# The sample's value block as fp32 on four column parts of TensorE, and GpSimd as the engine that normalizes the mLSTM's heads

## The chip, the core and the metric

The kernel runs on one core of one Trainium2 chip. The time is the device time of one execution in microseconds (us), as a median over runs. A core has TensorE (PE; its weight loads are listed apart, as PEld), VectorE (DVE), ScalarE (ACT), GpSimd (POOL) and SyncE (SP), which here issues the DMAs. Each engine works through its own instructions in a fixed order and waits on semaphores for the others.

## What is computed

The reference is one inference step of two trunk layers on a prompt of 1024 tokens and a sample block of 32 tokens, of width 1024. Layer 0 is an mLSTM mixer and an MLP, layer 1 chunk-band attention and an MLP. The change lies in layer 0's mixer, which has 4 heads with keys of 128 and values of 256:

```python
proj = u @ w_in
qk_pre = proj[..., :2 * QK_A]
v = proj[..., 2 * QK_A:2 * QK_A + V_A]
...
h, C, n, m = mlstm_scan(q, k, v, ig, lf, C0, n0, m0, chunk_len)
mu = h.mean(-1, keepdims=True)
var = jnp.square(h - mu).mean(-1, keepdims=True)
h = (h - mu) * lax.rsqrt(var + HEAD_NORM_EPS) * mhn_g
h = h.reshape(Bsz, S, V_A) * jax.nn.sigmoid(o_pre)
return h @ w_out, conv_new, C, n, m
```

Prompt and sample have states of their own, but share the weights, and so the kernel projects all 1056 tokens together.

## The kernel before

**Precision.** Most products run in fp32r, a faster form of fp32 on TensorE, on operands split into a high and a low part: `split` (line 87) casts on ScalarE (L89) and subtracts on VectorE (L90). A product then takes three matmuls, high by high, high by low and low by high. The modulated input u is kept in this way in the tile U, all channels of the high part, then of the low part, and 96 columns of zeros behind.

**Weights.** `wtile` loads 512 rows of a weight into a raw tile, of which there are three in a ring (`raw_tile`, line 84), by a DMA on SP's queue, and splits it into a w tile, of which there are six. A raw tile is free for the next load when both parts of the split have read it.

**Values.** The tokens are nine tiles: eight of 128 tokens of the prompt, and the sample's 32. `v_chunk` makes one eighth of a tile's product: the stationary operand is a block of u (128 channels by 128 tokens), the moving one 256 columns of the split weight, and three matmuls (L487 to L489) go into a PSUM bank. So a tile takes 24 matmuls. The sample's tile takes them too: its 32 tokens are read with the next 96 columns as a block of 128, and only 32 rows of the result are used. `v_out` copies the bank to a tile vt on ScalarE (L494). The nine vt tiles of a head reuse those of the head before. Head 0's values are made in `v_first` with 264 columns, of which the last eight are the gates. Those of heads 1 to 3 are made in `v_proj`, which loads both weight halves, then makes tile by tile, and calls `after(t)` behind each.

**The mLSTM.** `mlstm(h, ...)` is a generator that works in visits. It runs through the head's nine chunks (eight of the prompt, and the sample as chunk 8) while the next head's projections are made. In visit i, `scores(i)` makes S and the transposed keys, the decay weights W, the product sT (VectorE), the weighted keys kw (ScalarE) and the scaled queries qc (GpSimd, L675). `values(i - 1)` makes num (L686, L688) and the new state from cu (L690), takes the statistics of num on VectorE, and copies num to a tile hn on ScalarE (L708). After each third chunk, `scales` works out for three chunks together a scale and a shift, in some 13 short VectorE instructions on 128x3 (L715 to L727) with two on ScalarE between, and ScalarE applies them to the three hn tiles (L731). `heads(c)` transposes hn on TensorE (hT, L738) and copies it to G. `state_out` stores the final states. The heads of a trio are transposed in the visit behind the one that normalized them, and in the next.

**The order of work.** The projections call `flow.tick` behind each unit of theirs (`after_qk`, `tick`), and each tick makes the next visit of the mLSTM and the next step of other running tasks. For head 1 these are four ticks in `qk_proj` and nine in `v_proj`, for heads 2 and 3 six and nine; the last head's visits run in the twelve ticks of `o_proj([0, 1])`. The same ticks drive `ada_wide`, which works through the adaLN weights on VectorE (L279 and others) in steps. The order in which an engine meets its instructions is near the one in which they are written, but not equal to it: a scheduler puts ready instructions ahead of others that it expects to wait. So TensorE's transposes, say, stand between matmuls of a value tile.

**The conditioning vector** lies in cs, 32 columns for each of 8 blocks of channels, of which two are used. At the start, L435 multiplies cs in fp32 by the adaLN weight on four column parts of TensorE: the four results, 32 rows each, lie one below the other in one PSUM bank.

## Time and profile before

| | |
|---|---|
| median of 3 runs | 2409.23 us (2408.87 to 2410.61) |
| the profiled execution | 2412.41 us |
| its span, first to last instruction | 2410.6 us |
| mean granted TensorE clock | 0.995 |

The profile is of one execution. Its page gives busy time by engine; other views group instructions by line, list who waited for whom, list instructions in order of time, and give busy time by stretches of the span. In these rows stand the line of the code, the engine, the operation, the tiles written and read (`out<-in`), their shapes, the count (`x72`) and, in brackets, the idle time ahead and what ended it. A matmul's length holds its latency, so that successive ones overlap; what one costs is the distance between starts. In rows of stretches the figure behind the stretch's length is the busy time of each engine with its count of instructions, then the granted clock, the DMA engines' busy share and their GB/s. A row of waits has the total in us, the count and the longest.

### The profile page before, as it was taken

The numbers are of one execution on the slowest core, as the hardware profiler recorded it, in microseconds if no ns is written. First come the engines' busy times: TensorE is split into PE (matmuls) and PEld (weight loads), VectorE is DVE, ScalarE is ACT, GpSimd is POOL, SyncE is SP. The second block draws the span as 40 slices with busy tenths as digits, with TensorE's granted clock in tenths as the row PEclk, the third lists the DMA queues.
The fourth block names the chain that finished last, engine by engine and source line by source line (L and its number), as shares of the span: only waits on it lengthen the run. The fifth ranks groups of instructions, "written<-read, shape, count | busy, mean of one in ns | idle before, by whom it ended". The sixth has DMA issues, their size and how long they took to land. (4 is left out here: it accounts for less than half of the span.)

```text
span 2410.6 us, 44188 instructions
## 1 busy us (share of the span) xinstructions
PE 2342.7 (97%) x17180; PEld 2250.4 (93%) x17180; DVE 1939.0 (80%) x3903; ACT 1206.0 (50%) x2454; POOL 168.1 (7%) x320
## 2 busy tenths in 40 slices
PE   7999999999999999999999999999999999899997
PEld 4999999999999999999999987789999999899997
DVE  4888766778788789989888777756998889888778
ACT  4565557278666630101147467773776777222212
POOL 0111100000000000000000224420000000000003
PEclk9999999999999999999999999999999999999999
DMA  8343222526566896675512330051486779976642
GB/s 302 120 131 103 78 89 66 177 91 206 184 198 200 279 336 230 252 261 215 183 56 89 82 93 1 10 140 59 165 278 211 259 278 335 355 256 236 224 146 73
DMA packets 284277, 424.64 MB, mean 176 GB/s; under 512 B 15384, under 2 KB 205228, under 8 KB 278948
## 3 DMA queue, kind: packets, MB, share of 16 engines
q1 hardware_dynamic: 279860, 391.48, 48.3%
q10 hardware_dynamic: 4208, 30.35, 3.1%
q8 instruction: 135, 2.21, 0.4%
q14 instruction: 74, 0.61, 0.1%
HBM read 305.96 MB, written 118.17 MB: 176 GB/s over the span
## 5 line engine op out<-in xcount | busy, mean ns | idle before, releaser
L1082 DVE SCALAR_TENSOR_TENSOR ACX<-dn,ada,ACX 128x264 f32<-128x264 f32 (+6 forms) x664 | 281.8, 447 | 83.2 <-PE dn L1452 41.1
L1452 PE MATMUL dn<-fx,wf_d 128*128 128x264 f32 x2016 | 254.1, 285 | 6.8 <-DVE ACX L1082 3.5
L1452 PEld LDWEIGHTS dn<-fx,wf_d 128*128 128x128 f32 x2016 | 248.8, 188 | 9.0 <-DVE ACX L1082 3.0
L89 ACT CAST w_dn<-raw_dn 128x1024 fp32r<-128x1024 f32 x36 | 37.7, 1050 | 282.1 <-DVE aw L279 136.9
L118 PE MATMUL dn<-hs,w_dn 128*128 128x384 f32 (+2 forms) x512 | 161.2, 315 | 0.0
L119 PE MATMUL dn<-hs,w_dn 128*128 128x384 f32 (+2 forms) x512 | 161.0, 315 | 0.0
L120 PE MATMUL dn<-hs,w_dn 128*128 128x384 f32 (+2 forms) x512 | 156.4, 314 | 1.3 <-DVE w_dn L90 1.3
L1317 PE MATMUL up<-TF,wf_u 128*128 128x264 f32 x1056 | 143.2, 285 | 3.8 <-ACT H L1320 3.8
L1317 PE MATMUL up<-U,wf_u 128*128 128x264 f32 x1056 | 140.3, 285 | 1.7 <-ACT H L1320 1.2
L1317 PE MATMUL up<-u,wf_u 128*128 128x264 f32 x1056 | 139.7, 285 | 1.3 <-ACT wf_u L89 0.7
L279 DVE SCALAR_TENSOR_TENSOR aw<-radw,cs,aw 128x512 f32<-128x512 f32 x196 | 139.5, 743 | 1.1 <-DMA radw<-in_w_ada_dram 1.1
L1317 PEld LDWEIGHTS up<-TF,wf_u 128*128 128x128 f32 x1056 | 134.4, 189 | 4.8 <-ACT H L1320 4.6
L1317 PEld LDWEIGHTS up<-U,wf_u 128*128 128x128 f32 x1056 | 133.0, 188 | 3.0 <-ACT H L1320 1.6
L1317 PEld LDWEIGHTS up<-u,wf_u 128*128 128x128 f32 x1056 | 132.9, 188 | 1.9 <-ACT wf_u L89 0.9
L118 PE MATMUL dn<-U,w_dn 128*128 128x384 f32 (+2 forms) x416 | 129.4, 312 | 0.6 <-DVE ada L304 0.6
L119 PE MATMUL dn<-U,w_dn 128*128 128x384 f32 (+2 forms) x416 | 129.4, 312 | 0.0
L120 PE MATMUL dn<-U,w_dn 128*128 128x384 f32 (+2 forms) x416 | 125.9, 313 | 0.6 <-DVE w_dn L90 0.5
L1817 ACT ACTIVATE p<-p,mx 128x576 f32<-128x576 f32 (+9 forms) x132 | 86.6, 657 | 27.5 <-DVE mx L1814 25.2
L120 PEld LDWEIGHTS dn<-hs,w_dn 128*128 128x128 f32 x512 | 96.0, 188 | 2.0 <-DVE w_dn L90 1.8
L118 PEld LDWEIGHTS dn<-hs,w_dn 128*128 128x128 f32 x512 | 96.5, 189 | 0.1
L119 PEld LDWEIGHTS dn<-hs,w_dn 128*128 128x128 f32 x512 | 96.6, 189 | 0.0
L90 DVE TENSOR_TENSOR HL<-H,HL 128x1056 fp32r<-128x1056 f32 x64 | 80.3, 1254 | 20.0 <-ACT HL L89 19.9
(403 smaller groups left out, 7111.0 us busy)
## 6 DMA issues: line engine op xcount, KB each, us to landing
hpl<-HL SPq DMA_DIRECT2D x144, 264.0 KB
rdn_u<-in_w_up_dram SPq DMA_DIRECT2D x64, 512.0 KB
hd<-HL SPq DMA_DIRECT2D x28, 1056.0 KB
fx<-hd SPq DMA_DIRECT2D x50, 528.0 KB
radw<-in_w_ada_dram SPq DMA_DIRECT2D x24, 1024.0 KB
hd<-HM SPq DMA_DIRECT2D x28, 792.0 KB
raw_up<-in_w_up_dram SPq DMA_DIRECT2D x40, 512.0 KB
raw_dn<-in_w_down_dram SPq DMA_DIRECT2D x36, 512.0 KB
```

The lines of the kernel that those rows point to most:

```text
L89: nc.scalar.copy(dst_h, src)
L90: (eng or nc.vector).tensor_sub(dst_l, src, dst_h.bitcast(F32))
L118: nc.tensor.matmul(ps, wh, mov(0, k), start=(k == 0), stop=False)
L119: nc.tensor.matmul(ps, wh, mov(1, k), start=False, stop=False)
L120: nc.tensor.matmul(ps, wl, mov(0, k), start=False, stop=(k == nk - 1))
L279: nc.vector.scalar_tensor_tensor(acc[cnd], raw[:, k], sc, acc[cnd], op0=ALU.mult, op1=ALU.add)
L1082: nc.vector.scalar_tensor_tensor(xs, ps[:, off + o:off + o + mm_], gate[:, fc, cnd:cnd + 1], xs, op0=ALU.mult, op1=ALU.add)
L1317: nc.tensor.matmul(p, self.ws[w][:, wl, k], moving(f, tp, xl, k), start=first and k + n_ == 0, stop=k == 3 and n_ == 2, skip_group_check=n ...
L1452: nc.tensor.matmul(p, ws[w][:, wl, k], t[:, s0, xl], start=first and k + n_ == 0, stop=k == kg - 1 and n_ == 2, skip_group_check=not first)
L1817: nc.scalar.activation(z, z, AF.Exp, bias=mx[:, 0:1], scale=-1.0, accum_out=mx[:, 1:2])
```

## The change

For heads 1 to 3 the sample's values are no longer made from the split operands. The high and low parts of the sample's u are added once (`us`, on VectorE, behind head 0's values) into 32 further columns of cs, and `v_sample` multiplies them by the raw weights in fp32, as soon as a half of them is loaded and ahead of the split: four matmuls a half, each on one column part of TensorE, with 32 tokens stationary and 256 columns moving. The bank then holds four partial sums of 32 rows; ScalarE copies the first to vt, and VectorE adds the other three. These values stand ahead of the head's eight other tiles, in two vt tiles of their own. The ninth `after` follows the eighth at once.

Head 0's sample tile still uses the split operands, but with 32 tokens stationary, and so U loses its 96 columns of zeros. GpSimd applies scale and shift to hn in place of ScalarE. Each transposition stands one visit later, and within its visit ahead of `values`; the generator has 13 visits in place of 12. The constant `ones_d`, which the layer norms use, is made later, in another pool.

```diff
-            between()
+            between(raw)
         split(w[:, 0], w[:, 1], raw, eng)
...
-    cs = cp.tile([P, KC, 32], F32, name="cs")
+    cs = cp.tile([P, KC, 2 + TS], F32, name="cs")
+    us = cs[:, :, 2:]
...
-    U = upool.tile([P, 2 * UF + 96], F32R, name="U")
-    nc.vector.memset(U[:, 2 * UF:].bitcast(F32), 0.0)
+    U = upool.tile([P, 2 * UF], F32R, name="U")
...
     def v_chunk(ps, ws, t, k):
         w = ws[k // 4]
         n = w.shape[-1]
-        uh, ul = uap(0, k, t * P, P), uap(1, k, t * P, P)
+        m = P if t < NT - 1 else TS
+        uh, ul = uap(0, k, t * P, m), uap(1, k, t * P, m)
+        ps = ps[:m]
...
+    def v_sample(us, ps, half, raw):
+
+        for k in range(4):
+            nc.tensor.matmul(ps[32 * k:32 * k + 32, :256], us[:, 4 * half + k], raw[:, k], start=(half == 0),
+                             stop=(half == 1))
+
     def v_out(ps, h, t):
         m = P if t < NT - 1 else TS
-        vt = A.tile([P, 258], F32, tag="vt", name=f"vt_{h}_{t}", bufs=9)
+        vt = A.tile([P, 258], F32, tag="vt", name=f"vt_{h}_{t}", bufs=8) if m == P else \
+            A.tile([P, 258], F32, tag="vs", name=f"vt_{h}_{t}", bufs=2)
         nc.scalar.copy(vt[:m, :256], ps[:m, :256])
+        if m < P and h:
+            for q in range(1, 4):
+                nc.vector.tensor_add(vt[:m, :256], ps[32 * q:32 * q + m, :256], vt[:m, :256])
...
     def v_proj(h, after):
-        ws = [v_weight(h, half) for half in range(2)]
+        ps = mmt(f"v_{h}_s")
+        ws = [v_weight(h, half, lambda raw: v_sample(us, ps, half, raw)) for half in range(2)]
+        vs = v_out(ps, h, NT - 1)
         vts = []
-        for t in range(NT):
+        for t in range(NT - 1):
...
-        return vts
+        after(NT - 1)
+        return vts + [vs]
...
-                nc.scalar.activation(hn[:L], hn[:L], AF.Identity, bias=sm[:L, i, 7:8], scale=sm[:L, i, 6:7])
+                nc.gpsimd.tensor_scalar(hn[:L], hn[:L], sm[:L, i, 6:7], sm[:L, i, 7:8], op0=ALU.mult, op1=ALU.add)
...
-        for i in range(NT + 3):
+        for i in range(NT + 4):
             if i < NT:
                 scores(i)
+            if i >= 5 and i % 3 != 1:
+                for c in (i - 5, i - 4) if i % 3 == 2 else (i - 4,):
+                    heads(c)
             if 1 <= i <= NT:
                 values(i - 1)
             if 2 <= i < NT + 2:
                 state_out(i - 2)
-            if i >= 4 and i % 3:
-                for c in (i - 4, i - 3)[:3 - i % 3] if i % 3 == 1 else (i - 3,):
-                    heads(c)
             yield
...
+    uv = U.rearrange("p (i k t) -> p i k t", i=2, t=T)[:, :, :, TP:].bitcast(F32)
+    nc.vector.tensor_add(us, uv[:, 0], uv[:, 1])
...
+    ones_d = T_.tile([P, P], F32R, name="ones_d")
+    nc.vector.memset(ones_d.bitcast(F32), 1.0 / D)
```

## The prediction

> **What bounds the kernel now.** I read the totals first, then the stretches, then TensorE's waits. Heads are counted from 0, as in the names.

> ```profile
> span 2410.6 us, 44188 instructions
> PE 2342.7 (97%) x17180; PEld 2250.4 (93%) x17180; DVE 1939.0 (80%) x3903; ACT 1206.0 (50%) x2454; POOL 168.1 (7%) x320
> ```

> TensorE is busy for 97% of the span. The change touches the projections and the mLSTM, which end at about 390 us; so the next view is busy time by stretches.

> ```profile
> core 0: us, PE busy (x) PEld busy (x) DVE busy (x) ACT busy (x) POOL busy (x), PEclk, DMA share, GB/s
> 35.00:130.00 95.00, 92.20 (x610) 88.22 (x611) 81.02 (x157) 64.26 (x143) 13.90 (x30) 0.96 0.42 132
> 130.00:180.00 50.00, 48.68 (x343) 45.06 (x342) 42.26 (x107) 28.80 (x81) 8.79 (x22) 1.00 0.49 152
> 180.00:230.00 50.00, 48.65 (x337) 44.90 (x336) 44.51 (x109) 29.24 (x90) 8.65 (x30) 1.00 0.33 106
> 230.00:280.00 50.00, 49.78 (x340) 48.27 (x340) 41.93 (x86) 26.55 (x71) 5.42 (x16) 1.00 0.26 77
> 280.00:390.00 110.00, 108.73 (x697) 101.34 (x696) 70.88 (x194) 66.13 (x178) 8.43 (x23) 1.00 0.30 93
> 390.00:2411.00 2021.00, 1974.37 (x14768) 1916.19 (x14767) 1650.50 (x3232) 983.97 (x1884) 121.75 (x187) 1.00 0.54 184
> ```

> TensorE binds before 390 us and after it (1974 of 2021 us), where its order is unchanged. What TensorE saves early is thus saved at the end; what only ScalarE or GpSimd saves is not. The waits of TensorE and of its weight loads (PEld) between 35 and 390 us:

> ```profile
> PE hT L738 <- ACT hn L731: 3.5, 4, 1.3
> PE ae_ps L577 <- ACT stk L570: 2.4, 1, 2.4
> PE v L487 <- ACT U L378: 0.9, 1, 0.9
> PEld hT L738 <- ACT hn L731: 6.5, 11, 1.5
> ```

> Only one of them belongs to the change: the transposes hT wait for the heads hn that ScalarE normalizes (L731). One of the four of 3.5 us, by TensorE's timeline (start, length, and in brackets the idle time before it):

> ```profile
> 154.40 0.28 PE L487 MATMUL v<-w_v,U 128*128 128x256 f32 x1
> 155.87 0.44 PE L738 MATMUL hT<-ident,hn 128*128 128x128 f32 x2 [1.19 <-ACT hn L731]
> ```

> **The change part by part.** *Removed matmuls.* Heads 1 to 3 lose 3 x 24 = 72 fp32r matmuls of the sample's block. In the timeline 21 such matmuls start from the first to the last of these rows:

> ```profile
> 133.51 0.28 PE L487 MATMUL v<-w_v,U 128*128 128x256 f32 x1
> ...
> 135.87 0.28 PE L489 MATMUL v<-w_v,U 128*128 128x256 f32 x1
> ```

> That is 2.36 / 20 = 0.118 us each (the 0.28 is latency), so 72 x 0.118 = 8.5 us less.

> *Added matmuls.* TensorE at the start of head 2's values, before (v_2_0 is its first tile, num and cu the mLSTM of head 1):

> ```order
> L686 MATMUL num_1_4_2321<-vt_1_4_1705,sT_1_4_2220 128x257
> L688 MATMUL num_1_4_2321<-ct_1_3_2231,qc_1_4_2222 128x257
> L690 MATMUL cu_1_4_2324<-vt_1_4_1705,kw_1_4_2224 128x257
> L487 MATMUL v_2_0_2348<-w_v2_0_2340,U_136 128x256
> L488 MATMUL v_2_0_2348<-w_v2_0_2340,U_136 128x256
> ```

> And now (v_2_s is the sample's block, from the unsplit weights):

> ```order
> L699 MATMUL num_1_4_2306<-vt_1_4_1710,sT_1_4_2205 128x257
> L701 MATMUL num_1_4_2306<-ct_1_3_2216,qc_1_4_2207 128x257
> L703 MATMUL cu_1_4_2309<-vt_1_4_1710,kw_1_4_2209 128x257
> L494 MATMUL v_2_s_2319<-raw_v2_0_2320,cs_87 32x256 x4
> L494 MATMUL v_2_s_2319<-raw_v2_1_2329,cs_87 32x256 x4
> L487 MATMUL v_2_0_2344<-w_v2_0_2322,U_134 128x256
> ```

> Eight fp32 matmuls, four column parts each half, now stand ahead of the tiles. The nearest rows are four fp32 matmuls on four parts at the start (L435), 512 wide; the code issues 32 of them and the trace has 64, two instructions for each. The last two lines count them as they run, in two short stretches:

> ```profile
> L435 PE MATMUL ada<-rada,cs x64: 592/617/1062, 9.2 to 32.2; 128*32 128x512 f32 x64
> ...
> 24.83 1.06 PE L435 MATMUL ada<-rada,cs 128*32 128x512 f32 x8
> ...
> 25.00:25.05 0.05, 0.05 (x4) 0.00 (x0) 1.00 1.13 250
> ...
> 25.60:25.65 0.05, 0.05 (x4) 0.00 (x0) 1.00 0.91 268
> ```

> Eight instructions start at 24.83 and end 1.06 us later, and four run at any time: four parts at once, in two rounds. At 256 wide a matmul has two passes of some 0.215 us (num, 257 wide, 0.44 us for two, below): 0.43 us for a half's four. In head 1 the first of the four stands apart, with num and cu between, so there are 7 rounds: 7 x 0.43 = 3.0 us. One after another would be 24 x 0.43 = 10.3 us.

> *Change of shape.* The sample's own mLSTM chunk shows what 32-wide shapes cost among wide ones; the first two rows are an ordinary chunk:

> ```profile
> 150.63 0.59 PE L686 MATMUL num<-vt,sT 128*128 128x257 f32 x2
> 151.07 0.60 PE L688 MATMUL num<-ct,qc 128*128 128x257 f32 x2
> 151.50 0.38 PE L690 MATMUL cu<-vt,kw 128*128 128x257 f32 x1
> ...
> 158.81 0.62 PE L686 MATMUL num<-vt,sT 32*32 32x257 f32 x2
> 159.36 0.62 PE L688 MATMUL num<-ct,qc 128*32 128x257 f32 x2
> 159.91 0.38 PE L488 MATMUL v<-w_v,U 128*128 128x256 f32 x1
> 160.22 0.70 PE L690 MATMUL cu<-vt,kw 32*128 32x257 f32 x2
> 160.85 0.33 PE L747 MATMUL co<-ident,ct 128*128 128x128 f32 x1
> ```

> Two num, one v and one cu take 2.04 us here, against 3 x 0.43 + 0.118 = 1.41: 0.63 us over five changes of shape, 0.12 us each. The change adds 14: two round each head's v_s, two more in head 1, and six in head 0, whose sample tile is now 32 wide instead of padded to 128 and stands in three runs among the wide tiles. 14 x 0.12 = 1.7 us; the bounds are 0 and 14 x 0.19 (the v row: 0.31 - 0.118) = 2.7 us. [...] No row shows an fp32r matmul 32 wide: 24 of them cost between nothing (0.118 as now; the same 264 columns stream, so no gain) and 24 x (0.55 - 0.118) = 10.4 us at the 32-wide num's price. I take nothing, since they keep their type and columns.

> *The normalization.* Each of 36 heads' tiles moves to GpSimd. Its like there is the second row; the third is the smallest VectorE read of PSUM of this width:

> ```profile
> L731 ACT ACTIVATE hn<-hn,sm 128x256 f32<-128x256 f32 x32 | 17.1, 592 | 7.7 <-DVE sm L727 7.6
> L1825 POOL TENSOR_SCALAR p<-p,mx 128x256 f32<-128x256 f32 x8 | 4.7, 599 | 4.9 <-DVE mx L1823 4.8
> L696 DVE COPY ct<-cu 128x257 f32<-128x257 f32 x4 | 1.7, 418 | 0.1
> ```

> ScalarE loses 36 x 0.59 = 21 us, off the path; GpSimd gains 36 x 0.60 = 22 us on some 45 of 355. One tile takes as long as before, so hn is ready no earlier: it mostly waited for VectorE's scales (7.6 us). What counts is where hT now stands. Before, the stalled place (head 0, chunk 3, in head 1's tiles):

> ```order
> L487 MATMUL v_1_5_1744<-w_v1_1_1421,U_136 128x256
> L738 MATMUL hT_0_3_1672<-ident_64,hn_0_3_1482 128x128 x2
> L488 MATMUL v_1_5_1744<-w_v1_1_1421,U_136 128x256
> L489 MATMUL v_1_5_1744<-w_v1_1_1421,U_136 128x256
> L738 MATMUL hT_0_4_1676<-ident_64,hn_0_4_1542 128x128 x2
> ```

> And now:

> ```order
> L682 MATMUL S_0_8_1723<-ident_64,y_4_1038 32x128
> L699 MATMUL num_0_7_1740<-vt_0_7_748,sT_0_7_1664 128x257
> L751 MATMUL hT_0_3_1732<-ident_64,hn_0_3_1495 128x128 x2
> L701 MATMUL num_0_7_1740<-ct_0_6_1675,qc_0_7_1666 128x257
> L751 MATMUL hT_0_4_1736<-ident_64,hn_0_4_1555 128x128 x2
> L703 MATMUL cu_0_7_1743<-vt_0_7_748,kw_0_7_1668 128x257
> ```

> Here a chunk's S and num have come between the last tile and hT, and the stall should go. It isn't so everywhere. Head 1's first trio stood behind 36 matmuls of tiles after its chunk's cu, 36 x 0.118 = 4.2 us:

> ```order
> L489 MATMUL v_2_1_2416<-w_v2_0_2340,U_136 128x256
> L738 MATMUL hT_1_0_2240<-ident_64,hn_1_0_2030 128x128 x2
> L487 MATMUL v_2_1_2416<-w_v2_1_2345,U_136 128x256
> L488 MATMUL v_2_1_2416<-w_v2_1_2345,U_136 128x256
> L738 MATMUL hT_1_1_2244<-ident_64,hn_1_1_2109 128x128 x2
> ```

> Now, at the same place in the program, it stands in the tile before, behind v_2_s and 8 matmuls, 0.86 + 0.94 = 1.8 us:

> ```order
> L488 MATMUL v_2_0_2344<-w_v2_0_2322,U_134 128x256
> L751 MATMUL hT_1_0_2298<-ident_64,hn_1_0_2015 128x128 x2
> L751 MATMUL hT_1_1_2302<-ident_64,hn_1_1_2094 128x128 x2
> L489 MATMUL v_2_0_2344<-w_v2_0_2322,U_134 128x256
> ```

> It comes 2.4 us sooner, and a visit's delay in the source has bought no cover there. On GpSimd's queue hn stands behind qc of a later chunk, which waits for num, and qc of the next chunk behind three hn (1.8 us); a visit, one tile's 24 matmuls (2.8 us) and one chunk (3 x 0.43), lasts over 4 us and covers that. The waits cost 3.5 us (PE rows) to 6.5 us (PEld rows); by starts the quoted one cost 1.47 - 0.118 = 1.35, not 1.19, so I put all at 4.5. Nothing to all of it may go; some places gain cover and some lose it, so I take half: 2.2 us.

> *At nothing.* Nine additions of 32x256 and one for the sample's sum, 10 x 0.42 = 4.2 us, lie in VectorE's idle time (7.7, 5.5, 8.1 us in the three stretches from 130); uncovered they cost 4.2. The raw weights are now held until v_s has read them, and SP's next loads queue behind:

> ```profile
> 98.77 1.05 ACT L89 CAST w_v<-raw_v 128x1024 fp32r<-128x1024 f32 x1 [2.26 <-PE qk L120]
> 127.22 0.36 PE L487 MATMUL v<-w_v,U 128*128 128x256 f32 x1
> ```

> Weights were in 28 us ahead of their first use; now the next head's still have eight tiles' time. The constants and pads that move are single short instructions.

> **Sum:** -8.5 + 3.0 + 1.7 - 2.2 = -6.0 us. The profiled execution (2412.41 us, span 2410.6) would go to 2406.4; it lies 3.2 us over the median of the runs, 2409.23, from which I forecast 2403.2.

> **Rivals.** [...] (B) The waits stay as long as they are, since hT is again put where hn is just ready: -3.8, 2405.4. For: head 1's trio. (C) The column parts run one after another: 7.3 us more, 2410.5; the L435 counts speak against. (D) Slower: GpSimd holds VectorE.

> ```profile
> 153.73 3.89 POOL L645 TENSOR_SCALAR_AFFINE_SELECT rc<-rc 128x1024 f32<-128x1024 f32 x2 [4.17 <-DMA rc<-rc_d]
> 153.85 1.06 DVE L727 SCALAR_TENSOR_TENSOR sm<-sm 128x3 f32<-128x3 f32 x1
> L727 DVE SCALAR_TENSOR_TENSOR sm<-sm 128x3 f32<-128x3 f32 x12 | 3.3, 273 | 0.1
> ```

> A 128x3 operation of 0.27 us took 1.06 under a GpSimd one. If each of the 27 normalizations of heads 0 to 2 holds VectorE for 0.60 us, 16.2 us and nine additions (3.8) meet 21 us of idle time from 130 to 280; if that lies in the wrong places, all 20 us reach TensorE through sT and the scales: 2423.2. It decides from 10.8 us (2414.0). Against: GpSimd's rows of 128x256 already run beside VectorE at 0.60. [...] (E) The 32-wide fp32r matmuls cost 10.4: 2413.6.

> **How the numbers follow.** Forecast 0.47, A 0.13, B 0.22, C 0.05, D 0.09, E 0.04. 0.2% (4.8 us) is about what a measurement of this kernel can tell: faster is under 2404.4. Forecast (0.45 of its 0.47) and A give 0.58; B, C, the rest of the forecast and half of E 0.31; D and half of E 0.11. The range 2399 to 2409 holds the forecast, B and most of A, 0.8.

> **What would show it.** v_s at four at once and 0.43 us a half; wide matmuls at 0.118 round head 0's 32-wide ones; hT waits near 2 us in sum; VectorE's idle time before 280 us reduced by less than 10 us. A stall of hT over 5 us, or waits of num for sT, would prove me wrong.

## The result and the profile after

| | before | after |
|---|---|---|
| median | 2409.05 us (6 runs, 2408.44 to 2414.3) | 2426.4 us (6 runs, 2417.14 to 2430.25) |
| ratio of the runs | | 1.0069 (95%: 1.0056 to 1.0081) |
| the profiled execution | 2412.41 us | 2430.25 us |

The change costs 16.6 us (13.5 to 19.5, from the ratio), where 6 us less were forecast. The six times of after also spread over 13 us, and go with the mean granted clock of the execution: 2430.25 us at 0.990, 2417.14 us at 0.995. Three runs of the experiments below took 3572 to 10342 us (two of no_adds, one of split_trio); they count in the medians and not in the ratios.

The totals of after's page. TensorE has less to do than before and is busy for 6 us more, and the span is 18 us longer: some of the time is idle, and some of the busy time is slow.

```profile
span 2428.5 us, 44193 instructions
PE 2348.8 (97%) x17156; PEld 2248.7 (93%) x17156; DVE 1940.3 (80%) x3912; ACT 1190.4 (49%) x2418; POOL 194.0 (8%) x356
```

Busy time by stretches (engines in the order PE, PEld, DVE, ACT, POOL, then the granted clock):

```profile
130.00:180.00 50.00, 45.67 (x316) 40.55 (x315) 40.69 (x103) 23.99 (x71) 15.03 (x32) 0.97 0.44 136
180.00:230.00 50.00, 46.75 (x316) 43.37 (x315) 39.96 (x98) 24.96 (x75) 12.91 (x29) 0.97 0.27 81
230.00:280.00 50.00, 47.64 (x313) 44.12 (x311) 37.15 (x86) 21.45 (x66) 10.35 (x27) 1.00 0.30 97
280.00:390.00 110.00, 105.37 (x666) 96.53 (x666) 79.18 (x199) 56.67 (x153) 18.82 (x39) 0.94 0.32 99
```

TensorE was busy for 48.68 of 50 us from 130 on, and for 108.73 of 110 from 280 on, always at a clock of 1.00; now it idles for 2 to 5 us in each stretch, and in three of the four the clock is lowered too. Its waits between 35 and 390 us (sum, count, longest):

```profile
PEld hT L751 <- POOL hn L744: 18.0, 19, 2.8
PE hT L751 <- POOL hn L744: 10.0, 10, 1.4
PE hT L751 <- ACT w_o L89: 2.6, 1, 2.6
```

These are the transposes again, which the change was expected to relieve: 3.5 us before, now 10.0, and 2.6 at a place where the row names ScalarE's w_o only because that ended last; the weight loads' row has the same wait (2.8) for hn. How hn comes late is seen at 207 us, by the timelines of VectorE, GpSimd and TensorE:

```profile
173.29 0.17 DVE L740 SCALAR_TENSOR_TENSOR sm<-sm 128x3 f32<-128x3 f32 x1
173.63 1.61 POOL L744 TENSOR_SCALAR hn<-hn,sm 128x256 f32<-128x256 f32 x3 [6.17 <-DVE sm L740]
174.25 0.98 PE L751 MATMUL hT<-ident,hn 128*128 128x128 f32 x4 [1.38 <-POOL hn L744]
...
207.56 0.15 DVE L740 SCALAR_TENSOR_TENSOR sm<-sm 128x3 f32<-128x3 f32 x1
207.63 1.31 DVE L624 SCALAR_TENSOR_TENSOR y<-qkp,pt,y 128x1059 f32<-128x1059 f32 x1
207.81 3.18 POOL L744 TENSOR_SCALAR hn<-hn,sm 128x256 f32<-128x256 f32 x2 [0.40 <-DVE sm L740]
209.25 1.31 DVE L624 SCALAR_TENSOR_TENSOR y<-qkp,pt,y 128x1059 f32<-128x1059 f32 x1
209.42 0.44 PE L751 MATMUL hT<-ident,hn 128*128 128x128 f32 x2 [1.10 <-POOL hn L744]
211.04 0.69 PE L751 MATMUL hT<-ident,hn 128*128 128x128 f32 x2 [1.19 <-POOL hn L744]
```

At 173 us VectorE is done with the scales and quiet, and three tiles take 1.61 us. At 207 us VectorE goes on with the convolution (y, L624, 1.31 us each), and two tiles take 3.18 us: each ends about 0.4 us behind the end of a y (208.94 and 210.56), and each time TensorE has stood still for over a microsecond. Both y take 1.31 us, the median of all 24, while the two tiles take 1.55 and 1.64 us for 0.55: here GpSimd is held by VectorE, and the forecast's rival D had it the other way round. It is so in the whole stage: 28 of the 36 tiles take 0.54 to 0.68 us, the other eight 0.98 to 1.66, and all eight lie beside an instruction of VectorE on y, ada_acc or w_o, where of the 28 a single one does (at 157 us, beside ada_acc for 0.20 us). By what means VectorE holds GpSimd no run shows.

Then the clock. The stretches behind two of the stalls:

```profile
172.00:174.00 2.00, 0.87 (x6) 0.55 (x4) 1.28 (x7) 0.00 (x0) 0.36 (x1) 1.00 0.91 325
174.00:176.00 2.00, 1.66 (x9) 1.13 (x10) 0.18 (x1) 0.90 (x3) 1.25 (x3) 1.00 0.44 170
176.00:178.00 2.00, 2.00 (x9) 2.00 (x9) 1.37 (x3) 0.20 (x2) 0.00 (x0) 0.60 0.00 0
178.00:180.00 2.00, 2.00 (x9) 2.00 (x8) 1.50 (x3) 1.10 (x3) 0.00 (x0) 0.55 0.00 0
180.00:182.00 2.00, 2.00 (x14) 2.00 (x13) 2.00 (x4) 0.00 (x0) 0.00 (x0) 1.00 0.00 0
...
300.00:302.00 2.00, 1.06 (x6) 0.98 (x6) 1.50 (x2) 0.63 (x2) 1.97 (x3) 0.50 0.17 20
310.00:312.00 2.00, 2.00 (x11) 2.00 (x11) 1.28 (x5) 0.00 (x0) 0.00 (x0) 0.50 0.40 112
312.00:314.00 2.00, 2.00 (x16) 2.00 (x15) 0.00 (x0) 0.63 (x3) 0.00 (x0) 0.77 0.00 0
```

After the 1.38 us at 174.25 TensorE is granted half its clock from 176.4 to 179.8 us; behind the 2.6 us and through the 0.9 us around 300, from 299.3 to 312.9 us. A wide matmul's pitch there, over 18 of them:

```profile
308.68 0.41 PE L489 MATMUL v<-w_v,U 128*128 128x256 f32 x1
...
312.52 0.41 PE L489 MATMUL v<-w_v,U 128*128 128x256 f32 x1
```

That is 3.84 / 18 = 0.213 us, against 0.118. If TensorE's busy time in each microsecond is multiplied by what the clock lacks of 1 there, after loses 12.8 us in this way between 35 and 455 us, all of it ahead of the first matmul of the output product (op_a).

The first profile of before is a poor measure: its 2412.41 us are above the median. A second profile of it (before_again, below) took 2409.27 us, and is the reference from here on. There op_a starts at 419.7 us, and in the same stretch TensorE idles for 7.7 us and loses 1.7 to the clock; after has 436.7, 18.7 and 12.8. So the 17.0 us up to op_a are 11.0 of idle time and 11.1 of clock, less the 4.7 by which the work itself shrank (8.5 - 3.8, below): 17.4. Of the idle time, 9.0 us are more waits of hT (12.9 against 3.9); of the clock, 9.4 us lie behind three of these waits, and 1.7 at 36 us, ahead of the first hT, where before_again has the same wait for U (0.9 us) and no fall. From op_a to the last matmul it is 1980.5 us against 1976.5, another 4.0. These 21.0 us are more than the 16.6, since after's profile is the slowest of its six runs.

### The profile page after: what moved, and what is told of

Its sections match the earlier page's. It is cut to its first block, busy times and chain, and to the rows that moved or that the text cites. A ratio compares the mean times of both kernels' runs of the same rounds, so it can differ in the third digit from the quotient of the medians.

```text
span 2428.5 us, 44193 instructions
## 1 busy us (share of the span) xinstructions
PE 2348.8 (97%) x17156; PEld 2248.7 (93%) x17156; DVE 1940.3 (80%) x3912; ACT 1190.4 (49%) x2418; POOL 194.0 (8%) x356
## 5 line engine op out<-in xcount | busy, mean ns | idle before, releaser
L89 ACT CAST w_dn<-raw_dn 128x1024 fp32r<-128x1024 f32 x36 | 37.7, 1051 | 284.6 <-DMA raw_dn<-in_w_down_dram 132.7
L120 PE MATMUL dn<-hs,w_dn 128*128 128x384 f32 (+2 forms) x512 | 156.3, 314 | 1.3 <-DVE w_dn L90 1.3
L120 PE MATMUL dn<-U,w_dn 128*128 128x384 f32 (+2 forms) x416 | 125.8, 313 | 1.4 <-DVE w_dn L90 1.4
L120 PEld LDWEIGHTS dn<-hs,w_dn 128*128 128x128 f32 x512 | 95.9, 188 | 2.0 <-DVE w_dn L90 1.8
L1778 POOL TENSOR_TENSOR x<-x,kvss 128x1024 f32<-128x1024 f32 (+1 forms) x9 | 18.5, 2057 | 988.0 <-DVE QO L1731 948.2
```

Of the source, the lines that this page charges most:

```text
L89: nc.scalar.copy(dst_h, src)
L120: nc.tensor.matmul(ps, wl, mov(0, k), start=False, stop=(k == nk - 1))
```

## The experiments

Theory G: GpSimd's hn come late, TensorE waits for them, and its clock is lowered behind the waits. Rivals: V, the visit is at fault; P, the column parts are; L, GpSimd holds VectorE.

**One part at a time.** The changed kernel with one line undone (act_norm), and each part alone on the kernel before:

```diff
 act_norm
-                nc.gpsimd.tensor_scalar(hn[:L], hn[:L], sm[:L, i, 6:7], sm[:L, i, 7:8], op0=ALU.mult, op1=ALU.add)
+                nc.scalar.activation(hn[:L], hn[:L], AF.Identity, bias=sm[:L, i, 7:8], scale=sm[:L, i, 6:7])
 parts_only: act_norm with the visits of before
 pool_only: before with the first of these two lines
 late_only: before with the visits of after
```

> The changed kernel with the normalization back on ScalarE; column parts and the later visit stay. Theory G (GpSimd: its tiles of hn come late, TensorE waits for them at hT, and its clock is halved for some us behind such a wait): the waits of hT for hn fall from 12.9 us to under 4.5, the time lost to a halved clock from 12.8 us to about 3, and the time is 2403 to 2408. Rival V (the visit: the transposes stand in a worse place whichever engine normalizes): the waits stay at 10 us or more and the time above 2418. Rival P (the column parts and the shapes take what they cost, not the waits): above 2418 too, with few waits of hT.

> The kernel before with the sample's values on four column parts alone: ScalarE normalizes, the transposes in their old visits. Theory G: -8.5 us of matmuls and +3 to +5 of v_s and drains with the waits as before: 2404 to 2407. Rival V: the same, and well under act_norm. Rival P: 2415 or more.

> The kernel before with GpSimd in place of ScalarE in one line, nothing else. Theory G: hn is late at the old places too; waits of hT of 10 us or more, drops of the clock behind them, 2418 to 2430. Rival V: GpSimd alone does no harm, 2407 to 2412.

> The kernel before with the transposes one visit later and ahead of the values, nothing else. Theory G: the waits of hT do not grow, 2406 to 2411. Rival V: waits of 8 us or more, 2416 or more.

| | median us | ratio to before (95%) | hT for hn | clock | op_a | op_a to end |
|---|---|---|---|---|---|---|
| before_again | | | 3.9 | 1.7 | 419.7 | 1976.5 |
| pool_only | 2426.38 | 1.0073 (1.0059 to 1.0087) | 13.8 | 6.8 | 435.6 | 1974.3 |
| late_only | 2404.9 | 0.9987 (0.9978 to 0.9996) | 3.1 | 1.7 | 417.3 | 1976.7 |
| parts_only | 2414.52 | 1.0024 (1.0014 to 1.0034) | 6.0 | 3.4 | 420.0 | 1980.4 |
| act_norm | 2412.4 | 1.001 (1.0001 to 1.0018) | 6.0 | 0.0 | 418.4 | 1982.4 |

(us; hT for hn from TensorE's waits, clock as worked out above, op_a its first matmul, end the last matmul.) The waits of pool_only, of late_only and of parts_only:

```profile
PE hT L738 <- POOL hn L731: 13.8, 13, 1.9
```

```profile
PE hT L738 <- ACT hn L731: 3.1, 4, 1.0
```

```profile
PE hT L751 <- ACT hn L744: 6.0, 6, 2.0
```

The first is one line of before changed, and the whole loss of after is there (+17.6 us), with its waits. G holds against V; the later visit (late_only, second row) gains 3.1 us. But the column parts alone (third row) are no gain of 4 us but a loss of 5.8, so parts_only and act_norm both missed what G expected, and P is half right. The parts add up: 5.8 - 3.1 = 2.7 for act_norm (2.4 measured), and GpSimd's line on top of it 14.0 (2426.4 - 2412.4).

**What about GpSimd?** pool_idle leaves the normalization on ScalarE and gives GpSimd the same work for nobody; late2_pool gives the transposes a second visit; split_trio gives GpSimd a third of the tiles:

```diff
 pool_idle: late_only, behind the activation
+                jk = A.tile([P, 256], F32, tag="jk", name=f"jk_{h}_{c0}_{i}", bufs=1)
+                nc.gpsimd.tensor_scalar(jk[:L], cs.rearrange("p k c -> p (k c)")[:L], sm[:L, i, 6:7], sm[:L, i, 7:8],
+                                        op0=ALU.mult, op1=ALU.add)
 late2_pool (late2_act: with the activation)
+            if i >= 6 and i % 3 != 2:
+                for c in (i - 6, i - 5) if i % 3 == 0 else (i - 5,):
+                    heads(c)
 split_trio: late_only
+                if i == 2:
+                    nc.gpsimd.tensor_scalar(hn[:L], hn[:L], sm[:L, i, 6:7], sm[:L, i, 7:8], op0=ALU.mult, op1=ALU.add)
```

> late_only (ScalarE normalizes), and beside it GpSimd makes for every tile the same multiplication and addition on 128x256, from a constant tile into a tile that nobody reads; head 0's sample tile is 32 wide and ones_d stands in the later pool, which makes the room. Theory G (hn itself comes late from GpSimd): no more than 2 us over late_only's 2404.9, 2403 to 2407. Rival L (GpSimd holds VectorE, my rival D of the prediction): 2412 or more.

> GpSimd normalizes, but the transposes stand two visits later than before, with five tiles of hn in place of four; no column parts; sample tile 32 wide. Theory G with lateness as its cause: the waits of hT fall from some 14 us (pool_only) to under 4, no halved clock behind them, 2402 to 2409. Rival L: the time stays at 2416 or more, or VectorE's waits take the place of hT's.

> As late2_pool, with ScalarE normalizing. Theory G: waits of hT under 2 us, 2400 to 2405, at least as fast as late_only (2404.9). Rival: the late transposes meet a new wait (tiles of hn not free for the copies of num), 2408 or more.

> late_only with GpSimd normalizing only the third tile of each trio and ScalarE the first two. Theory G (the first transposes wait for the first tile, and GpSimd's tiles come after one another): the first hT starts some 0.7 us behind the scales as in late_only, waits under 5 us, 2403 to 2408. Rival (any tile on GpSimd is late for its transpose): a third of the 18 us, 2409 to 2413.

pool_idle: 2407.26 us (ratio 0.9992, 0.9984 to 1.0001). The work is there, in both engines' groups (busy, mean ns of one, idle before), and the last row has TensorE's waits for hn:

```profile
L732 POOL TENSOR_SCALAR jk<-cs,sm 128x256 f32<-128x256 f32 (+1 forms) x36 | 26.5, 736 | 40.7 <-DVE sm L726 38.7
L730 ACT ACTIVATE hn<-hn,sm 128x256 f32<-128x256 f32 (+1 forms) x36 | 19.0, 590 | 8.6 <-DVE sm L726 8.6
PE hT L740 <- ACT hn L730: 1.8, 3, 1.0
```

GpSimd's 36 tiles are slowed as in after (736 ns in mean, for 0.55 us of a quiet one), and where TensorE doesn't wait for them the time is 2.4 us over late_only, not 18. G had allowed 2 us; the 0.4 more are within what the runs spread. L falls. late2_pool took 2414.34 us (1.0027, 1.0019 to 1.0036), 12 us under pool_only, but not the 2402 to 2409 expected; its waits halve, and its clock loses 4.8 us:

```profile
PE hT L737 <- POOL hn L730: 6.7, 8, 1.8
```

Why not more? In before the first hT of a trio starts 0.69 to 0.96 us behind the end of the last scale instruction in all twelve trios, that is, as soon as the first tile is normalized. In late2_pool, two visits later in the source, it starts 4.6 to 7.7 us behind in only five of twelve, and in the other seven 0.7 to 1.7 us behind. The scheduler puts the transposes where it expects hn to be ready, and the visit only bounds this. late2_act, 2407.46 us (0.9991, 0.9982 to 1.0), gains nothing on late_only: its 1.8 us of waits are as expected, its time is 2.6 us above late_only's, and above the 2400 to 2405 expected. split_trio, 2407.96 us (0.9994, 0.9985 to 1.0004), is 3.1 us over late_only, at the upper end of what G expected; of its 4.9 us of waits for hn only 1.0 are for GpSimd's tiles. The time doesn't tell the two readings apart.

**What about the column parts?** no_adds and no_sample take work away, sum_pe moves the sum to TensorE:

```diff
 no_adds: parts_only
-        if m < P and h:
-            for q in range(1, 4):
-                nc.vector.tensor_add(vt[:m, :256], ps[32 * q:32 * q + m, :256], vt[:m, :256])
 no_sample: parts_only
-        ps = mmt(f"v_{h}_s")
-        ws = [v_weight(h, half, lambda raw: v_sample(us, ps, half, raw)) for half in range(2)]
-        vs = v_out(ps, h, NT - 1)
+        ws = [v_weight(h, half) for half in range(2)]
+        vs = A.tile([P, 258], F32, tag="vs", name=f"vt_{h}_{NT - 1}", bufs=2)
+        nc.gpsimd.memset(vs[:TS], 1.0)
 sum_pe: act_norm, in place of the additions
+            pv = A.tile([P, 256], F32, tag="hn", name=f"pv_{h}", bufs=4)
+            nc.scalar.copy(pv, ps[:, :256])
+            ps = tpt(f"vsum_{h}")
+            nc.tensor.matmul(ps[:m, :256], sel, pv, start=True, stop=True)
```

> The column parts alone (as in parts_only), but without the three additions on VectorE that sum the four parts of each sample block; vt then holds one part of the sum. Theory A (VectorE has no room there: the additions I took for nothing are paid): 3 to 6 us under parts_only's 2414.5, so 2408.5 to 2411.5. Rival F (the matmuls removed were TensorE's work while it waited for the mLSTM, or the parts themselves cost more): within 2 us of parts_only.

> As parts_only, but the sample's values of heads 1 to 3 are left out: no matmuls of v_s, no copy, no additions; GpSimd fills the tile with ones. Theory R (TensorE binds, so removed matmuls come back in full): 8.5 us under before's 2408.7, 2399 to 2402. Rival F (part of them only filled TensorE's time while it waited for the mLSTM): 2404 or more.

> The changed kernel with ScalarE normalizing (as act_norm) and the four parts summed on TensorE in place of VectorE: ScalarE copies all 128 rows, one fp32 matmul of 32x256 with stacked identities sums them, ScalarE copies the result. Theory A (the additions take VectorE's time): 3 us or more under act_norm's 2412.4, 2405 to 2409. Rival: the longer path to the sample's values or the added matmuls (0.6 us a head) take it back, 2411 or more.

> The kernel before, unchanged, for a second profile: its first one, 2412.4, lies above the median of 35 runs, 2408.7. If the 3 us are chance in that execution, the stage of the MLP's first product (up) takes 347 to 348 us as in the kernels without column parts, not 351, and the kernels with column parts at 349 to 352 lose some 3 us there.

| | median us | ratio to before (95%) | hT for hn | clock | op_a | op_a to end |
|---|---|---|---|---|---|---|
| no_adds | 2411.15 | 1.0011 (1.0001 to 1.002) | 3.4 | 3.4 | 417.6 | 1979.7 |
| no_sample | 2404.23 | 0.9977 (0.9968 to 0.9987) | 3.7 | 0.0 | 408.9 | 1983.0 |
| sum_pe | 2409.99 | 1.0008 (0.9999 to 1.0016) | 4.5 | 1.7 | 417.6 | 1977.9 |

Without the additions the time falls by 3.4 us, near the 3.8 that nine at 0.42 are, and the waits of hT fall by 2.6 us (6.0 to 3.4): most of what they take is paid. With the sum on TensorE the time is 2.4 us under act_norm's, a little short of the 3 that A expected. no_sample tells most. The first matmul of op_a in before_again, and in no_sample:

```profile
419.74 0.44 PE L118 MATMUL op_a<-U,w_oa 128*128 128x384 f32 x1
```

```profile
408.86 0.45 PE L118 MATMUL op_a<-U,w_oa 128*128 128x384 f32 x1
```

By then it has gained 10.9 us, the 8.5 of the matmuls, 1.7 of clock and 0.7 more: up to here R is right and F wrong. But the time falls by only 5.5 (3.1 to 7.7), to where F had put it: from op_a on it is 6.5 us slower than before_again, though TensorE's instructions stand in the same order there. before_again itself did not show what was expected of it: its stage up takes 350 us, not 347, and the stage alone is no mark of the column parts.

**Where do they lose it again?** Over all profiles, op_a to end takes 1974.3 to 1979.0 us in the eleven of kernels without column parts (1976.6 in mean), and 1977.9 to 1983.0 in the seven with them (1980.9). The two groups overlap, and two profiles of one kernel differ by 1.8 us (parts_only) and 2.5 (before). Three kernels try the layout that the latter share:

```diff
 cs_wide: late_only
-    cs = cp.tile([P, KC, 32], F32, name="cs")
+    cs = cp.tile([P, KC, 34], F32, name="cs")
 narrow_all: before, with U, v_chunk and ones_d of after
 vs_tiles: narrow_all with the visits of after, and
-        vt = A.tile([P, 258], F32, tag="vt", name=f"vt_{h}_{t}", bufs=9)
+        vt = A.tile([P, 258], F32, tag="vt", name=f"vt_{h}_{t}", bufs=8) if m == P else \
+            A.tile([P, 258], F32, tag="vs", name=f"vt_{h}_{t}", bufs=2)
```

> late_only with cs widened from 32 to 34 columns a block, as in the changed kernel, the new columns unused: everything behind it in the memory moves by 64 bytes a partition, and the stride of the conditioning vector changes. Theory M (the layout slows the later stages): 3 us or more over late_only's 2404.9, and the stages behind 420 us 3 us longer. Rival: no change, 2403 to 2407, so the later loss goes with the column parts themselves.

> The kernel before with the sample's tile of all four heads 32 tokens wide instead of padded to 128, U without its pad, ones_d in the later pool. If 32-wide fp32r matmuls cost what the wide ones do and the layout is of no account: 2407 to 2411, as before. At 0.55 us each (the bound in the prediction) 96 of them would cost 41 us. Theory M for this half of the layout: 2412 or more.

> parts_only once more, for a second profile. If the later stages' loss belongs to the kernel, the MLP's first stage (up) takes 350 to 353 us again and what follows 420 us is 3 to 5 us longer than in before_again; if it is chance of one execution, it varies by as much between the two profiles.

> ScalarE normalizes, transposes one visit later, sample tile 32 wide, and the value tiles split as in the changed kernel: eight vt and two of their own for the sample, filled as before from the split operands. If this piece of the layout makes the later loss: what follows the first output product takes 1979 us or more and the time is 2409 or more. If not: under 1979, 2404 to 2408 as late_only and cs_wide.

| | median us | ratio to before (95%) | op_a | op_a to end |
|---|---|---|---|---|
| cs_wide | 2407.08 | 0.9996 (0.9987 to 1.0004) | 417.6 | 1975.5 |
| narrow_all | 2409.07 | 1.0 (0.9991 to 1.0008) | 419.0 | 1977.5 |
| vs_tiles | 2405.56 | 0.9985 (0.9977 to 0.9993) | 416.9 | 1977.6 |
| parts_again (one run) | 2416.43 | | 421.1 | 1982.2 |

None of the three pieces of the layout makes the loss by itself, and the second profile of parts_only repeats it (1980.4, now 1982.2). So some 4 us behind op_a go with the column parts, in no_sample too, which has no matmul of them but all of their layout. All pieces of the layout together, with the values made as before, were not tried. Why stays open.

No kernel tried that does the whole work beats late_only and vs_tiles, 3.1 us (1.0 to 5.3) and 3.6 us (1.7 to 5.5) under before: the later visit alone, with ScalarE.

## Why the prediction was wrong

- **Removed matmuls, -8.5:** right. no_sample has them, and 1.7 of clock, at op_a; but "What TensorE saves early is thus saved at the end" failed: in the profiles 6.5 of its 10.9 us are lost behind op_a, and the runs kept 5.5. Why is not shown.
- **Added matmuls, 3.0, and changes of shape, 1.7:** nearly right. Head 1's and head 2's halves, from the first to the next tile, in after's timeline:

```profile
128.24 0.62 PE L494 MATMUL v_s<-raw_v,cs 128*32 128x256 f32 x2
...
131.29 0.39 PE L487 MATMUL v<-w_v,U 128*128 128x256 f32 x1
...
206.10 1.07 PE L494 MATMUL v_s<-raw_v,cs 128*32 128x256 f32 x16
207.10 0.39 PE L487 MATMUL v<-w_v,U 128*128 128x256 f32 x1
```

 Head 2's take 1.00 us with both changes of shape, where 2 x 0.43 + 2 x 0.12 = 1.10 were reckoned; head 1's, 3.05 us less 3 x 0.43 for num and cu between, 1.76 against 1.77. Head 3's are as head 2's: 3.8 in all. What the expectation of parts_only calls drains are these changes of shape; no run shows that TensorE drains at one, only what it cost, by these two sums 0.07 us each at head 2 and 0.12 at head 1. Rival C is out. Head 0's changes of shape cost nothing: 18 matmuls, 32 wide, and the next wide one,

```profile
67.29 0.28 PE L487 MATMUL v<-w_v,U 128*32 128x264 f32 x1
...
69.46 0.28 PE L487 MATMUL v<-w_v,U 128*128 128x264 f32 x1
```

 stand 2.17 us apart, 0.121 each, against 0.122 for the 12 wide ones ahead of them (1.46 us). narrow_all, with 96 of them, takes the time of before: rival E is out.
- **The waits of hT, -2.2:** the step that failed, with the sign wrong: 12.9 us in after against 3.9 in before_again. It rested on "One tile takes as long as before", a price taken from a row of the attention. After's tiles (ns, least, median and most), and GpSimd's qc in the mLSTM of before:

```profile
L744 POOL TENSOR_SCALAR hn<-hn,sm x36: 544/555/1661, 146.7 to 393.7; 128x256 f32<-128x256 f32 x32, 32x256 f32<-32x256 f32 x4
L675 POOL TENSOR_TENSOR qc<-y,rc x32: 240/458/1479, 105.0 to 354.3; 128x128 f32<-128x128 f32 x28, 128x32 f32<-128x32 f32 x4
```

 Most of the tiles are as quick as ScalarE's 0.59 us, and the slowest, beside VectorE, takes three times as long. The second row shows that before had it already: half the size took up to 1.48 us, and that one lies beside y. The tiles of a trio follow one another, and TensorE's order put the first transposes right behind the scales already in before. So there was no half to win, and each delay was paid. Of the places quoted, head 0's chunk 3 came out as forecast, with no wait:

```profile
157.29 0.60 PE L699 MATMUL num<-vt,sT 128*128 128x257 f32 x2
157.72 0.38 PE L751 MATMUL hT<-ident,hn 128*128 128x128 f32 x2
```

 But head 0's other trios now wait, for 1.31 us at 147.85 and 1.38 at 174.25, and head 1's first trio, for which the prediction saw no cover, waits twice for over a microsecond, at 209 and 211.
- **A term that was missing: the clock.** Half of the 22 us of idle and slow time up to op_a is TensorE at half clock, and 9.4 us of that lie behind stalls of hT. The rows of before had shown it once, 0.96 in the stretch from 35 to 130 us that was quoted, behind the 2.4 us wait for ae_ps. A wait was priced at its length.
- **At nothing:** the additions cost 3.4 us (no_adds), though VectorE idled for 21 us from 130 to 280 before. That idle time did not shrink but grew to 32 us.
- **Rival D** named 2423.2 us, near the result, by luck, for a reason that does not hold: pool_idle keeps all of GpSimd's work beside VectorE and is 2.4 us over late_only. No wait of num for sT appears. In after's rows it is GpSimd's tile that grows beside VectorE, from 0.55 to as much as 1.66 us. **B** was right about the order: hT is again put where hn is just ready. It left the waits at their length.
- "A stall of hT over 5 us, or waits of num for sT, would prove me wrong": neither came as one stall; the many of 0.4 to 2.6 us did it. The mark was badly chosen: the sum of the waits, named as near 2 us and measured as 12.9, was the better one.

## What to carry to other kernels

Before a step on a chain that TensorE waits for is moved to an engine that looks idle, ask which of its neighbours can hold that engine, and price the tile by the worst rows that the engine has in that stage (here 1.48 us for half the size), not by a mean from another (0.60). A stall of TensorE can cost more than its length: behind the 1.38 us at 174 us came 3.4 us at half clock, another 1.7 us. Count what the lowered clock takes. And a delay in the source is no cover where a scheduler sorts by the time that it expects: in late2_pool, two visits later, seven of twelve trios still started 0.7 to 1.7 us behind the scales.

## What the runs showed of the hardware

```profile
145.67:149.08 3.41, 1.99 (x15) 1.53 (x14) 1.79 (x5) 0.58 (x2) 2.99 (x6) 1.00 0.00 0
172.97:176.39 3.42, 2.05 (x12) 1.52 (x13) 0.98 (x5) 0.96 (x3) 1.61 (x3) 1.00 0.57 222
176.39:179.80 3.41, 3.41 (x13) 3.41 (x12) 2.28 (x5) 1.25 (x3) 0.00 (x0) 0.50 0.00 0
295.85:299.27 3.42, 0.96 (x9) 0.75 (x7) 3.06 (x8) 2.06 (x5) 2.36 (x3) 1.00 0.87 298
```

 Of all such stretches at full clock between 30 and 455 us in the 18 traces, half clock followed 21 of the 22 in which TensorE was busy for less than half, 6 of the 23 at 0.5 to 0.6, and none of the 2163 above; the first two rows, at 0.58 and 0.60, went different ways. Where the grid lies differs between executions: the fall behind the wait for ae_ps began at 91.61 us in before and at 94.47 in after, 2.86 apart and no multiple of 3.413. This wait of some 2.5 us brought half clock in 16 profiles and none in act_norm and no_sample. So the clock column of one profile is in part luck.
- An fp32r matmul with 32 tokens stationary costs what one with 128 does (0.121 us at 264 columns), and changing between the two cost nothing: 2.17 us for 18, two changes among them. Between fp32 matmuls on column parts and their neighbours a change cost 0.07 us (head 2) to 0.12 us (head 1), an estimate from 1.00 and 1.76 us less the rounds at 0.43.
